# Two merge gates moved ahead of the GLA norm, a low-rank product moved behind the recurrence, another pace for w_ada, and a first expert turn of 64 slots with 21 first blocks

## The chip, the cores and the metric

The kernel runs on one core of one Trainium2 chip. The metric is the device time of one execution in microseconds; of several runs the median is taken. The core has a tensor engine (PE, with its weight loads as PEld), a vector engine (DVE), a scalar engine (ACT), GpSimd (POOL) and a sync engine (SP). SP issues nearly all weight transfers, POOL those of w_ada. A queue works its instructions in order, so one that waits holds up all behind it.

## The reference

Two layers of a decoder for 256 tokens of width 1024. Each has a token mixer and a channel mixer, both with a norm that a conditioning vector c scales and shifts (adaLN: six vectors per layer from `silu(c) @ w_ada`). The mixer runs a gated linear attention branch (GLA) and an RWKV-7 branch side by side and merges them with two sigmoid gates per channel:

```python
p = h @ w_in
y_a = _gla_branch(pq, pk, pv, pg, pa, ...)     # log_a from (pa @ alpha_up); o * rsqrt(mean(o*o)); silu(pg); @ w_o
y_b = _rwkv7_branch(p_rwkv, ...)               # recurrence over the tokens
merged = sigmoid(gate_a) * y_a + sigmoid(gate_b) * y_b
return merged @ w_out
```

`pa` has 16 columns: it is the low-rank gate input of the GLA decay. Layer 0's channel mixer is a dense SwiGLU of width 2816, layer 1's a mixture of 8 experts of width 3584 with the best 2 for each token. A token's expert output is weighted by a softmax over the two. A last norm closes the program.

## The kernel before, in words

All values are kept transposed, channels on partitions and the 256 tokens along the free axis. A weight block is 128 x 2048 f32, 1 MiB, and is called raw; `project` (L382) splits each 128 x 1024 half of it into hi and lo (L367 on ACT, L369 on DVE) and runs three matmuls per chunk of 128 (L392 to L394) into a PSUM tile pj, of which there are three. A projection over 1024 channels is 24 matmuls.

The order of the work comes from three sources. In the mixers and the dense layer a planner orders each engine's queue: it takes the instructions in the order of the text as priority, but pulls ahead what is ready when an engine would otherwise stand still. SP's queue is written out by hand there (LOADS), in the order of the text. In the expert stage the queues of PE, DVE, ACT and SP are all in the order of the text; a small clock (`tick`, `after`) places the side work between the products.

In `mixer` the text goes: projections W and G (L624 to L629), the low-rank gate product `pas` from wpa (L630 to L637: one split and 24 matmuls with 16 output columns), the low-rank RWKV products (L640 on), the RWKV projections, the recurrence (L776 to L817), its output yh and yl (up to L842), then the GLA branch: `decays()` (L865, reads pas at L871), `values` (L846), the heads and gates in the order of GATE_SEQ, the norm of the GLA output (`rsq` at L985, spread over partitions at L348, products at L992 to L994), four units of w_og (L996 to L1000), and eight merge steps (L1009 to L1019), each with a projection of a gate tile 38 + i, a tanh, a projection of w_or, and the merge; at last w_out.

The vectors from w_ada are made beside all this. A unit is 128 x 1024 of w_ada; POOL fetches it into one of two araw buffers (L230), DVE adds it to an accumulator (L254, L256), and after eight units two closing steps (`late`) finish a vector. `pace(n)` counts the chunks of each projection and calls `feed` for one unit or closing step each time PACE of the phase is full: 13 in mixer 0, 9 in the dense layer, 28 in mixer 1. `hold` stops it until the ninth entry of GATE_SEQ. `need(0, 4)` ahead of w_out in mixer 0 calls `feed` until vectors 2, 3 and 4 are there.

In `moe` the eight experts run in turns. Turn 0 is always expert 0, since its blocks are fetched before the router is known; the others are sorted by their token counts. A turn is small (CAP = 64 slots) or large (128 slots), by SMALL: before, turns 0, 2, 4, 6 are large and 1, 3, 5, 7 take the four experts with the fewest tokens. A turn has 7 steps j, each of 2 blocks for w1, w3 and w2: 42 blocks. A small turn multiplies the raw block in fp32 (L1404, L1423) with two column halves; a large one splits each half block (L1187, L1188) and runs three products (L1408 to L1410, L1426 to L1428). A large block is handed back when it is split, a small one when its products are done. `fetch` (L1163) issues blocks on SP: first the list FIRST, 18 places (15 raw ones and three that other tiles take over later: acts, late, y), then one for each block handed back while fewer than 15 are live. The expert order reaches SP through a register load (L1312). If a small turn has more than 64 tokens, or a large one more than 128, a branch at the end (`spill`) runs all experts again.

The places lie where mixer 1's tiles were, so the first transfers wait until these are done.

Of the kernel before, what the change touches and what calls it, by code (L numbers as in the profile page):

```python
# [9 lines left out]
F32 = mybir.dt.float32  # L10
F32R = mybir.dt.float32r
I32 = mybir.dt.int32
BF16 = mybir.dt.bfloat16
AF = mybir.ActivationFunctionType
# [4 lines left out]
P = 128  # L19
T = 256  # L20
# [37 lines left out]
NPRE = len(PRE)  # L58


RANK = [7, 0, 4, 1, 5, 2, 6, 3]
SMALL = [False, True] * 4
CAP = 64
NSMALL = sum(SMALL)
GROUPS = [(None, 0), (1, 2), (3, 4), (5, 6), (7, None)]


def constants():
# [367 lines left out]
WOUT = ((2, 'BT'), (3, 'TT'))  # L436
MOE_BUFS = 15
PLACES = [f"raw{i}" for i in range(6)] + ["acts", "late"] + [f"raw{i}" for i in range(6, MOE_BUFS)]
FIRST = ["acts", "late"] + [f"raw{i}" for i in (6, 7, 8, 4, 5, 12, 13, 14, 9, 10, 11, 2, 3, 1, 0)] + ["y"]
PACE = (13, 9, 28)  # L440
PACED_FROM = 8
ARAW_BUFS = 2
ARAW_WIDE = 6
# [86 lines left out]
def mixer(k, l):  # L530
# [10 lines left out]
    def g1():  # L541
        return made.pop() if made else dp.tile([P, T], F32, name="g1", bufs=G_BUFS)
# [45 lines left out]
    def tile_of(i):  # L588
        w = unit(i // 2)
        return w[:, (i % 2) * 1024:(i % 2) * 1024 + 1024]  # L590
# [36 lines left out]
    gds = shift(proj(1), 13)  # L627
    nc.scalar.activation(sgd, gds, AF.Tanh, scale=0.5)
    nc.vector.tensor_scalar(sgd, sgd, 0.5, 0.5, ALU.mult, ALU.add)  # L629
    hi, lo = k.split(wpa)  # L630
    pap = k.pj()
    for kc in range(KC):
        s = slice(kc * 16, kc * 16 + 16)
        nc.tensor.matmul(pap[:16, :T], hi[:, s], hh[:, kc, :], start=kc == 0, stop=False)
        nc.tensor.matmul(pap[:16, :T], hi[:, s], hl[:, kc, :], start=False, stop=False)
        nc.tensor.matmul(pap[:16, :T], lo[:, s], hh[:, kc, :], start=False, stop=kc == KC - 1)
    nc.scalar.activation(pas, pap[:16, :T], AF.Copy)  # L637


    PP, IP, AI, KK = [big[:, i * 1024:(i + 1) * 1024].rearrange("p (h t) -> p h t", h=4) for i in range(4)]  # L640
    for hp in range(2):
# [200 lines left out]
        nc.vector.tensor_tensor(yl[:, ht], u, yh[:, ht].bitcast(F32), ALU.subtract)  # L842

    def values(half):  # L846
        pv = [k.pj(), k.pj()]
# [134 lines left out]

    oh = dp.tile([P, 8, T], F32R, name="BK")
    ol = dp.tile([P, 8, T], F32R, name="vt")
    gsr = k.rsq(gss, 8, 1.0 / 256, 1e-5)  # L985
    for h in range(4):
        pb = k.pg()
# [19 lines left out]
        late[u] = dp.tile([P, 2048], F32, name=n)  # L1007
        nc.sync.dma_start(late[u], A["wout"][l, u])
    for i in range(8):  # L1009
        gb = k.project(tile_of(38 + i), act)  # L1010
        tb = g1()
        nc.scalar.activation(tb, gb, AF.Tanh, scale=0.5)
        if i % 4 == 0:
            w = k.raw(A["wor"][l, i // 4])
        py = k.project(w[:, (i % 4) * 512:(i % 4) * 512 + 512], (yh, yl))
        nc.vector.scalar_tensor_tensor(tb, tb, 1.0, py, ALU.add, ALU.mult)
        nc.vector.tensor_tensor(tb, tb, ta[:, i], ALU.add)
        nc.scalar.activation(mh[:, i], tb, AF.Copy, scale=0.5)
        nc.vector.scalar_tensor_tensor(ml[:, i], tb, 0.5, mh[:, i].bitcast(F32), ALU.mult, ALU.subtract)  # L1019
# [114 lines left out]
def moe(k, l, out):  # L1134
# [16 lines left out]
    todo = [o + (h,) for o in order for h in range(2)]  # L1151
    live, blocks, expert = [], [], [0]

    once = {n: sp.tile([P, 2048], F32, name=n) for n in PLACES}
    once["y"] = dp.tile([P, 2048], F32, name="y")
    slots = list(FIRST)

# [18 lines left out]
    def prepare(eng=nc.vector):  # L1176

        block = blocks[0]
        w, at, _ = block
        q = len(part)  # L1180
        s = slice(q * SUB, (q + 1) * SUB)
        last = q == 2048 // SUB - 1
        if SMALL[at[0]]:
            ready.append((w[:, s], None, at + (q,), block if last else None))
        else:
            hi, lo = [sp.tile([P, SUB], F32R, name=n, bufs=SPLIT_MOE) for n in ("hi", "lo")]
            nc.scalar.activation(hi, w[:, s], AF.Copy)  # L1187
            eng.tensor_tensor(lo, w[:, s], hi.bitcast(F32), ALU.subtract)  # L1188
            ready.append((hi, lo, at + (q,), None))
        part.append(q)  # L1190
        if last:
            part.clear()
            blocks.pop(0)
            if not SMALL[at[0]]:
                done(block)
# [6 lines left out]
            held[n] = sp.tile([P, 4, 512], kind, name=n)  # L1202
        return held[n]

    turns = [0, 0]

    def room():
        turns[0] += 1
# [82 lines left out]
    def sort():  # L1291

        by = lambda a: a[:, None, :].to_broadcast([P, NE, NE])
        of = lambda a: a[:, :, None].to_broadcast([P, NE, NE])
        p, w = perm[:, 0], perm[:, 1]

        def ranks():
            nc.vector.scalar_tensor_tensor(key, n8, 8.0, k.k("keyc"), ALU.mult, ALU.add)
            nc.vector.tensor_tensor(w, of(key), by(key), ALU.is_gt)
            nc.vector.tensor_reduce(rank, w, AX.X, ALU.add)  # L1300
            nc.vector.tensor_tensor(p, by(rank), of(k.k("seq")), ALU.is_equal)
            nc.vector.tensor_tensor(w, p, by(iota[:, :NE]), ALU.mult)
            nc.vector.tensor_reduce(idx, w, AX.X, ALU.add)
            nc.vector.tensor_copy(idxi, idx)

        def turned(src, dst):
            for tt in range(2):
                nc.vector.tensor_tensor(w, p, by(src[:, tt]), ALU.mult)
                nc.vector.tensor_reduce(dst[:, tt], w, AX.X, ALU.add)

        def loads():
            _, v = nc.values_load_multi_w_load_instructions(idxi[0:1, 1:NE], engines=[mybir.EngineType.SP], min_val=0,  # L1312
                                                            max_val=NE - 1)
            expert.extend(v)

        def excess():
            nc.vector.tensor_scalar(more, rank, NSMALL - 0.5, float(P - CAP), ALU.is_le, ALU.mult)
            nc.vector.tensor_tensor(n8, n8, more, ALU.add)
            nc.vector.tensor_reduce(cnt, n8, AX.X, ALU.max)
            nc.vector.tensor_copy(cnti, cnt)  # L1320

        return [ranks, loads, lambda: turned(posm, posm_s), lambda: turned(comb, comb_s), excess]
# [40 lines left out]

    def places(g):

        xs = dp.tile([P, KC, CAP], F32, name="xs") if GROUPS[g][0] is not None else None
        xl = [dp.tile([P, KC, P], F32R, name=n) for n in ("xh", "xl")] if GROUPS[g][1] is not None else None
        return xs, xl

# [225 lines left out]
    with tc.manual_schedule(engines=ORDERED | LOADS):  # L1595
        y = choose()
        idle = k.pj()
        busy(IDLE[0])
        pp = place()
        busy(IDLE[1])  # L1600
        for c in range(3):
            rows_of(c, y)
        rows_of(0, y, True)
        nc.vector.tensor_tensor(posm, posm, pp[:, 0:2 * NE].rearrange("p (a b) -> p a b", a=2), ALU.add)
        new = slots_of(0)
        nc.vector.tensor_copy(n8, pp[:, 2 * NE:3 * NE])
        rows_of(1, y, True)
        rows_of(2, y, True)
        to = places(0)
        for kc in range(KC):  # L1610
            gather(0, new[1], kc, to, k.pj if kc % 4 > 1 else k.pg)
        weigh()
        after(BACK, lambda: back(*new))
        for n, f in enumerate(sort()):
            after(SORT + n, f)
        group = new, to
        for e in range(NE):
            i = 0 if SMALL[e] else 1
            if e and i == 0:
                group = nxt  # L1620
            (_, _, gs, PT), (xs, x2) = group
            for j in range(NJ):
                ph = [k.pj()]
                up(e, j, 0, ph[0], x2 if i else xs)
                act, steps = hidden(e, ph)
                delay = DELAY
                if (e, j) == (NE - 1, NJ - 1):
                    delay, last = LAST, gains()
                after(delay[0], steps[0])
                ph.append(k.pj())  # L1630
                up(e, j, 1, ph[1], x2 if i else xs)
                for d, f in zip(delay[1:], steps[1:]):
                    after(d, f)
                if i == 1 and e < NE - 1:
                    g = e // 2 + 1
                    if j == NJ - 2:
                        new = slots_of(g)
                        after(BACK, lambda: back(*new))
                    if j == NJ - 1:
                        nxt = new, places(g)  # L1640
                        for kc in range(KC):
                            after(kc * 2048 // SUB // 4, lambda kc=kc, g=g, n=nxt: gather(g, n[0][1], kc, n[1]))
                if pend:
                    down(*pend[:4])
                    if pend[4]:
                        for d, f in in_turn(pend[0], *scatter(pend[0], pend[2], *pend[4])):
                            after(d, f)
                if j == 0:
                    py = []
                pend = (e, j, py, act, (gs[:, i:i + 1], PT, i) if j == NJ - 1 else None)  # L1650
        while tasks:
            tick()
        down(*pend[:4])
        banks = iter((k.pg, k.pg, k.pj, k.pj))
        finish(scatter(pend[0], pend[2], *pend[4], lambda: next(banks)()), *last)
# [168 lines left out]
```

## Time and profile before

| what | value |
|---|---|
| median of 3 runs | 1780.85 us (1779.85 to 1782.62) |
| profiled execution | 1777.78 us |
| its span, first to last instruction | 1776.0 us |
| granted TensorE clock, mean | 0.977 of 2.4 GHz |
| busy: PE, PEld, DVE, ACT, POOL | 96%, 79%, 65%, 47%, 3% |
| moved by DMA | 520.92 MB, mean 293 GB/s |

The profile is one execution on the chip. "Busy" of an engine is the union of its instructions; matmuls overlap, so the sum of their durations is more. A number behind a bar or in brackets is the engine's idle time just ahead of an instruction, with what ended it. PEclk is the granted clock as a share of 2.4 GHz. Mixer 0 ends near 357 us, the dense layer near 567, mixer 1 near 900; the expert stage follows.

### The profile page before, as it was taken

The page shows a single profiled execution, that of the slowest core. Times are in us where ns is not written, and L with a number is a line of the kernel's source. Part 1 is how long each engine was busy: PE and PEld are TensorE (multiplying, and loading weights), DVE is VectorE, ACT ScalarE, POOL GpSimd, SP SyncE. Part 2 cuts the span into 40 slices and gives each one's busy share as a digit, 9 for nine tenths or more (in the row PEclk, how much of TensorE's full clock was granted, in tenths as well). Part 3 has the DMA queues.
Part 4 walks back from the last instruction along what each step waited for, and adds up shares of the span by engine and source line. Part 5 has one row for each costly group of instructions (what it writes and reads, how often), then busy time and mean ns, then how long its engine had stood idle before and what let it go on. Part 6 is the DMA issues. An engine that isn't in the chain of part 4 may idle for free.

```text
span 1776.0 us, 30054 instructions
## 1 busy us (share of the span) xinstructions
PE 1703.6 (96%) x11915; PEld 1400.8 (79%) x11915; DVE 1161.7 (65%) x1783; ACT 838.2 (47%) x1214; POOL 50.3 (3%) x100
## 2 busy tenths in 40 slices
PE   7998989989999799999999999999999999999997
PEld 6987879989999688799977875688656876578754
DVE  3789577787876879466669950588407972289611
ACT  3653234454444743244547740477306771267501
POOL 0000010010100000000000000000000000000001
PEclk9999899999999899899989999999999999999999
DMA  9445257687874333225678989999999999999995
GB/s 347 158 165 190 73 182 259 249 287 304 314 267 145 110 129 119 73 96 190 261 307 311 366 314 421 421 421 421 418 420 421 421 421 416 421 421 421 420 421 214
DMA packets 79972, 520.92 MB, mean 293 GB/s; under 512 B 9520, under 2 KB 10160, under 8 KB 22352
## 3 DMA queue, kind: packets, MB, share of 16 engines
q1 hardware_dynamic: 67440, 476.14, 67.7%
q0 software_dynamic: 11232, 40.90, 6.7%
q8 instruction: 95, 1.56, 0.4%
q10 hardware_dynamic: 1152, 1.89, 0.3%
q14 instruction: 53, 0.43, 0.1%
HBM read 517.84 MB, written 1.05 MB: 292 GB/s over the span
## 4 chain that ended last, share of the span: by engine, by line
PE 76%; issue 8%; DMA 7%; DVE 6%; ACT 1%; POOL 0%; SPq 0%; ACTq 0%; POOLq 0%; DVEq 0%
PE pj L1404 11%; PE pj L392 7%; PE pj L393 7%; PE pj L394 7%; PE pc L1423 6%; PE pj L1408 5%; PE pj L1410 5%; PE pj L1409 5%; DMA araw<-wada 4%; PE pc L1426 3%; PE pc L1428 3%; PE pc L1427 3%; DMA raw<-moe 2%; PE pg L1453 1%; DVE lo L369 1%
## 5 line engine op out<-in xcount | busy, mean ns | idle before, releaser
L1188 DVE TENSOR_TENSOR lo<-raw,hi 128x1024 fp32r<-128x1024 f32 x330 | 396.1, 1223 | 85.0 <-ACT hi L1187 77.9
L1187 ACT ACTIVATE hi<-raw 128x1024 fp32r<-128x1024 f32 x330 | 347.5, 1059 | 128.1 <-PE pj L1409 80.0
L367 ACT ACTIVATE hi<-raw 128x1024 fp32r<-128x1024 f32 (+2 forms) x209 | 213.9, 1025 | 280.7 <-PE pj L393 207.6
L369 DVE TENSOR_TENSOR lo<-raw,hi 128x1024 fp32r<-128x1024 f32 (+2 forms) x209 | 246.5, 1181 | 77.5 <-ACT hi L367 73.9
L392 PE MATMUL pj<-hh,hi 128*128 128x256 f32 x992 | 289.9, 292 | 4.8 <-DVE t L418 3.4
L394 PE MATMUL pj<-hh,lo 128*128 128x256 f32 x992 | 285.9, 288 | 1.3 <-DVE lo L369 1.3
L393 PE MATMUL pj<-hl,hi 128*128 128x256 f32 x992 | 286.2, 289 | 0.0
L1404 PE MATMUL pj<-raw,xs 128*64 128x256 f32 x1792 | 201.4, 381 | 0.0
L392 PEld LDWEIGHTS pj<-hh,hi 128*128 128x128 f32 x992 | 191.2, 193 | 12.1 <-issue 4.8
L394 PEld LDWEIGHTS pj<-hh,lo 128*128 128x128 f32 x992 | 191.1, 193 | 2.5 <-DVE lo L369 1.8
L393 PEld LDWEIGHTS pj<-hl,hi 128*128 128x128 f32 x992 | 191.3, 193 | 2.2 <-issue 1.3
L1408 PE MATMUL pj<-hi,xh 128*128 128x512 f32 x448 | 181.3, 405 | 0.5 <-ACT hi L1187 0.5
L1410 PE MATMUL pj<-lo,xh 128*128 128x512 f32 x448 | 178.5, 398 | 2.0 <-DVE lo L1188 1.9
L1409 PE MATMUL pj<-hi,xl 128*128 128x512 f32 x448 | 177.7, 397 | 0.0
L1404 PEld LDWEIGHTS pj<-raw,xs 128*64 128x64 f32 x1792 | 125.8, 137 | 64.9 <-issue 4.7
L1448 DVE TENSOR_TENSOR late<-late,pj 128x512 f32<-128x512 f32 (+1 forms) x56 | 30.8, 550 | 207.6 <-PE pj L1404 201.0
L1410 PEld LDWEIGHTS pj<-lo,xh 128*128 128x128 f32 x448 | 84.5, 189 | 25.7 <-DVE lo L1188 5.4
L1423 PE MATMUL pc<-raw,as 128*64 128x512 f32 x448 | 102.2, 595 | 0.0
L1408 PEld LDWEIGHTS pj<-hi,xh 128*128 128x128 f32 x448 | 84.8, 189 | 21.2 <-ACT hi L1187 1.9
L1409 PEld LDWEIGHTS pj<-hi,xl 128*128 128x128 f32 x448 | 84.7, 189 | 18.7
L256 DVE SCALAR_TENSOR_TENSOR aacc<-araw,csg,aacc 128x1024 f32<-128x1024 f32 x70 | 89.6, 1280 | 8.0 <-DMA araw<-wada 7.5
L1426 PE MATMUL pc<-hi,acts 128*128 128x512 f32 x224 | 88.3, 394 | 0.0
(432 smaller groups left out, 2749.2 us busy)
## 6 DMA issues: line engine op xcount, KB each, us to landing
raw<-moe SPq DMA_DIRECT2D x333, 1024.0 KB, 18.6
raw<-win SPq DMA_DIRECT2D x43, 1024.0 KB, 5.0
araw<-wada POOLq DMA_DIRECT2D x78, 512.0 KB, 5.3
raw<-f SPq DMA_DIRECT2D x33, 1024.0 KB, 7.3
raw<-wv SPq DMA_DIRECT2D x8, 1024.0 KB, 4.8
raw<-wog SPq DMA_DIRECT2D x8, 1024.0 KB, 5.0
raw<-wad SPq DMA_DIRECT2D x6, 1024.0 KB, 7.1
raw<-wor SPq DMA_DIRECT2D x4, 1024.0 KB, 5.1
```

The lines of the kernel that those rows point to most:

```text
L367: nc.scalar.activation(hi[:, :w], src, AF.Copy)
L369: nc.vector.tensor_tensor(lo[:, :w], src, hi[:, :w].bitcast(F32), ALU.subtract)
L392: nc.tensor.matmul(o, hi[:, s], ah[:, kc, :], start=kc == 0, stop=False)
L393: nc.tensor.matmul(o, hi[:, s], al[:, kc, :], start=False, stop=False)
L394: nc.tensor.matmul(o, lo[:, s], ah[:, kc, :], start=False, stop=kc == nk - 1)
L1187: nc.scalar.activation(hi, w[:, s], AF.Copy)
L1188: eng.tensor_tensor(lo, w[:, s], hi.bitcast(F32), ALU.subtract)
L1404: nc.tensor.matmul(p[64 * n:64 * n + 64, :T], x[:, kc], hi[:, z * 512 + n * T:z * 512 + n * T + T], start=kc == 0, stop=kc == KC - 1)
L1408: nc.tensor.matmul(p, x[0][:, kc], hi[:, s], start=kc == 0, stop=False)
L1409: nc.tensor.matmul(p, x[1][:, kc], hi[:, s], start=False, stop=False)
L1410: nc.tensor.matmul(p, x[0][:, kc], lo[:, s], start=False, stop=kc == KC - 1)
L1423: nc.tensor.matmul(py[0][64 * n:64 * n + 64], act[:, a:a + CAP], hi[:, s], start=first, stop=last)
```

## The change

- `pas`, the low-rank gate product, moves from behind the projections W and G to behind yh and yl, ahead of `values` and `decays` in the text, in both mixers.
- Two of the eight merge gates (projection of tiles 38 and 39, and their tanh) move from the merge loop to ahead of the norm of the GLA output, in both mixers; so does the fetch of their unit, ahead of w_og's four on SP.
- PACE of mixer 0 goes from 13 to 10.
- Turn 0 becomes small: SMALL is true for turns 0, 1, 3, 5 and 7, and GROUPS, which pairs a small and a large turn for slots, places and gathers, is moved to match. Turn 1's tokens lie in a quarter of late, since turn 0's are still in use.
- The hi and lo tiles of the expert stage become three tiles hl0 to hl2 of the same total size, which serve as places for three more first blocks: 21 in place of 18.
- `excess` tests the ranks for the new set of small turns, with two more steps.

```diff
-SMALL = [False, True] * 4
+SMALL = [True] + [True, False] * 3 + [True]
-GROUPS = [(None, 0), (1, 2), (3, 4), (5, 6), (7, None)]
+GROUPS = [(0, None), (1, 2), (3, 4), (5, 6), (7, None)]
...
+FIRST = ["acts", "late"] + [f"raw{i}" for i in (6, 7, 8, 4, 5, 12, 13, 14, 9, 10, 11, 2, 3, 1, 0)] + ["y"] + [
+    f"hl{i}" for i in range(3)]
-PACE = (13, 9, 28)
+PACE = (10, 9, 28)
...
-    hi, lo = k.split(wpa)
-    pap = k.pj()
-    for kc in range(KC):
...
-    nc.scalar.activation(pas, pap[:16, :T], AF.Copy)
...
         nc.vector.tensor_tensor(yl[:, ht], u, yh[:, ht].bitcast(F32), ALU.subtract)
+    hi, lo = k.split(wpa)
+    pap = k.pj()
+    for kc in range(KC):
...
+    nc.scalar.activation(pas, pap[:16, :T], AF.Copy)
...
+    def merge_gate(i):
+        tb = g1()
+        nc.scalar.activation(tb, k.project(tile_of(38 + i), act), AF.Tanh, scale=0.5)
+        return tb
+
+    ahead = {i: merge_gate(i) for i in range(2)}
     gsr = k.rsq(gss, 8, 1.0 / 256, 1e-5)
...
-        gb = k.project(tile_of(38 + i), act)
-        tb = g1()
-        nc.scalar.activation(tb, gb, AF.Tanh, scale=0.5)
+        tb = ahead.pop(i) if i in ahead else merge_gate(i)
...
-    once = {n: sp.tile([P, 2048], F32, name=n) for n in PLACES}
+    once = {n: sp.tile([P, 2048], F32, name=n) for n in PLACES + [f"hl{i}" for i in range(SPLIT_MOE)]}
...
-            hi, lo = [sp.tile([P, SUB], F32R, name=n, bufs=SPLIT_MOE) for n in ("hi", "lo")]
+            hl = sp.tile([P, 2 * SUB], F32R, name=f"hl{turns[2] % SPLIT_MOE}")
+            turns[2] += 1
+            hi, lo = hl[:, :SUB], hl[:, SUB:]
...
-            nc.vector.tensor_scalar(more, rank, NSMALL - 0.5, float(P - CAP), ALU.is_le, ALU.mult)
+            nc.vector.tensor_scalar(more, rank, -5.0, None, ALU.add)
+            nc.vector.tensor_tensor(more, more, more, ALU.mult)
+            nc.vector.tensor_scalar(more, more, 2.0, float(P - CAP), ALU.is_ge, ALU.mult)
...
-        xs = dp.tile([P, KC, CAP], F32, name="xs") if GROUPS[g][0] is not None else None
+        xs = None
+        if g == 1:
+            xs = parts("late")[:, 3].rearrange("p (k n) -> p k n", k=KC)
+        elif GROUPS[g][0] is not None:
+            xs = dp.tile([P, KC, CAP], F32, name="xs")
...
-                if i == 1 and e < NE - 1:
+                if (i == 1 or e == 0) and e < NE - 1:
```

## Rows read from the trace of the kernel before

**Rows 1.** The page: engines' busy time, and GB/s in the 40 slices.
```profile
PE 1703.6 (96%) x11915; PEld 1400.8 (79%) x11915; DVE 1161.7 (65%) x1783; ACT 838.2 (47%) x1214; POOL 50.3 (3%) x100
...
GB/s 347 158 165 190 73 182 259 249 287 304 314 267 145 110 129 119 73 96 190 261 307 311 366 314 421 421 421 421 418 420 421 421 421 416 421 421 421 420 421 214
```

**Rows 2.** Windows, turns 0 to 2: length, busy by engine, PEclk, DMA share, GB/s.
```profile
916.20:1044.20 128.00, 124.14 (x562) 99.21 (x563) 107.60 (x132) 93.43 (x111) 0.00 (x0) 0.98 0.89 339
1044.20:1120.00 75.80, 75.80 (x566) 43.94 (x568) 12.76 (x21) 10.75 (x20) 0.00 (x0) 1.00 0.98 398
1120.00:1254.20 134.20, 132.83 (x622) 102.93 (x619) 109.61 (x115) 95.09 (x112) 0.00 (x0) 1.00 1.01 421
```

**Rows 3.** Windows by transfer: opening of the expert stage, steady part, tail.
```profile
898.30:1053.30 155.00, 148.20 (x711) 118.90 (x711) 126.26 (x187) 106.44 (x134) 0.00 (x0) 0.97 0.88 338
1053.30:1754.80 701.50, 697.57 (x4068) 480.14 (x4069) 373.54 (x416) 322.33 (x404) 2.90 (x8) 1.00 1.01 418
1754.80:1776.00 21.20, 11.44 (x84) 8.42 (x80) 6.01 (x18) 4.68 (x8) 2.19 (x3) 0.86 0.15 54
```

**Rows 4.** Timeline of SP's queue, and one row of ACT: start, us, instruction.
```profile
210.54 50.43 SPq L379 DMA_DIRECT2D raw<-wog  x4
...
898.26 8.90 SPq L1163 DMA_DIRECT2D raw<-moe  x10
...
905.25 2.04 ACT L1187 ACTIVATE hi<-acts 128x1024 fp32r<-128x1024 f32 x2
...
909.31 0.33 SPq L1163 DMA_DIRECT2D y<-moe  x1
924.60 136.51 SPq L1163 DMA_DIRECT2D raw<-moe  x45
```

**Rows 5.** Timeline of the tensor engine in both mixers; idle time ahead in brackets.
```profile
95.58 0.51 PE L858 MATMUL pj<-hi,hh 128*128 128x512 f32 x1
...
128.51 0.71 PE L904 MATMUL pg<-g,g 128*128 128x128 f32 x4
...
260.70 0.44 PE L278 MATMUL ada<-cst,sq 128*128 128x128 f32 x2 [1.23 <-ACT sq L273]
265.71 2.08 PE L348 MATMUL pg<-cst,rsq 128*128 128x128 f32 x8 [4.57 <-DVE rsq L341]
...
586.69 0.37 PE L634 MATMUL pj<-hh,hi 128*16 128x256 f32 x1 [7.81 <-DVE t L418]
...
811.55 0.62 PE L392 MATMUL pj<-BK,hi 128*128 128x256 f32 x3 [0.71 <-ACT BK L993]
```

**Rows 6.** Instructions of one line: SP's read of the order (L1312), block transfers (L1163).
```profile
L1312 SPq TENSOR_LOAD <-idxi x1: 1663/1663/1663, 934.5 to 934.5; - x1
...
DMA to landing us min/median/max: 5.0/18.6/20.8
```

**Rows 7.** Windows for the matmul's price and the granted clock.
```profile
930.00:940.00 10.00, 8.02 (x34) 5.45 (x34) 9.12 (x20) 6.61 (x7) 0.00 (x0) 1.00 0.34 116
...
264.70:271.60 6.90, 5.72 (x25) 5.43 (x26) 5.44 (x15) 2.43 (x6) 0.82 (x2) 0.51 1.01 419
...
400.00:500.00 100.00, 100.00 (x846) 98.37 (x846) 76.47 (x85) 43.72 (x59) 12.69 (x24) 1.00 0.84 316
```

**Rows 8.** Timeline of DVE in the mixers.
```profile
259.35 1.22 DVE L369 TENSOR_TENSOR lo<-raw,hi 128x1024 fp32r<-128x1024 f32 x1
...
290.31 1.28 DVE L256 SCALAR_TENSOR_TENSOR aacc<-araw,csg,aacc 128x1024 f32<-128x1024 f32 x1 [3.07 <-DMA araw<-wada]
...
576.20 1.28 DVE L256 SCALAR_TENSOR_TENSOR aacc<-araw,csg,aacc 128x1024 f32<-128x1024 f32 x1
```

**Rows 9.** Waits: engine and line waited for, us in total, times, longest.
```profile
POOL araw L230 <- DVE aacc L256: 108.2, 41, 10.6
```

**Rows 10.** Windows of the recurrences, instructions on the accumulators pj alone.
```profile
128.50:234.10 105.60, 56.81 (x349) 49.27 (x349) 4.22 (x10) 3.84 (x9) 0.92 0.41 140
672.90:758.80 85.90, 47.07 (x272) 38.55 (x270) 2.54 (x6) 3.44 (x8) 0.90 0.28 97
```

More of the change, by code (lines that the diff above doesn't have):

```diff
@@ L61 @@
 RANK = [7, 0, 4, 1, 5, 2, 6, 3]
-SMALL = [False, True] * 4
+SMALL = [True] + [True, False] * 3 + [True]
 CAP = 64
-NSMALL = sum(SMALL)
-GROUPS = [(None, 0), (1, 2), (3, 4), (5, 6), (7, None)]
+GROUPS = [(0, None), (1, 2), (3, 4), (5, 6), (7, None)]
 def constants():
@@ L438 @@
 PLACES = [f"raw{i}" for i in range(6)] + ["acts", "late"] + [f"raw{i}" for i in range(6, MOE_BUFS)]
-FIRST = ["acts", "late"] + [f"raw{i}" for i in (6, 7, 8, 4, 5, 12, 13, 14, 9, 10, 11, 2, 3, 1, 0)] + ["y"]
-PACE = (13, 9, 28)
+FIRST = ["acts", "late"] + [f"raw{i}" for i in (6, 7, 8, 4, 5, 12, 13, 14, 9, 10, 11, 2, 3, 1, 0)] + ["y"] + [
+    f"hl{i}" for i in range(3)]
+PACE = (10, 9, 28)
 PACED_FROM = 8
@@ L629, in mixer @@
     nc.vector.tensor_scalar(sgd, sgd, 0.5, 0.5, ALU.mult, ALU.add)
-    hi, lo = k.split(wpa)
-    pap = k.pj()
-    for kc in range(KC):
[L633 to L636, printed above, removed]
-    nc.scalar.activation(pas, pap[:16, :T], AF.Copy)
     PP, IP, AI, KK = [big[:, i * 1024:(i + 1) * 1024].rearrange("p (h t) -> p h t", h=4) for i in range(4)]
@@ L842, in mixer @@
         nc.vector.tensor_tensor(yl[:, ht], u, yh[:, ht].bitcast(F32), ALU.subtract)
+    hi, lo = k.split(wpa)
+    pap = k.pj()
+    for kc in range(KC):
+        s = slice(kc * 16, kc * 16 + 16)
+        nc.tensor.matmul(pap[:16, :T], hi[:, s], hh[:, kc, :], start=kc == 0, stop=False)
+        nc.tensor.matmul(pap[:16, :T], hi[:, s], hl[:, kc, :], start=False, stop=False)
+        nc.tensor.matmul(pap[:16, :T], lo[:, s], hh[:, kc, :], start=False, stop=kc == KC - 1)
+    nc.scalar.activation(pas, pap[:16, :T], AF.Copy)
     def values(half):
@@ L1203, in parts @@
         return held[n]
-    turns = [0, 0]
+    turns = [0, 0, 0]
     def room():
```

## The prediction

> **What bounds the kernel now.** I read the page's slices first, then the expert stage turn by turn, the transfers there, and the tensor engine's holes in the mixers. The tensor engine is busy for 96% of the span [rows 1], nearly everywhere, so its share does not say what ends last; the slices' GB/s do. From slice 25 on they stand at 416 to 421 but for the last, and lower and uneven before.
>
> In the expert stage the reader should compare two prices of a turn (one expert, 42 blocks of 1 MiB, 44.04 MB). A large turn (128 slots, hi/lo split, three products) takes 134.2 us of the tensor engine, a small one (64 slots, raw weights) 75.8 [rows 2]. From 1053.3 us to the last landing at 1754.8 the queue moves 418 GB/s [rows 3], so 42 blocks take 44.04 MB / 418 GB/s = 105.4 us. A pair takes 134.2 + 75.8 = 210.0 us of products and 210.8 of transfer: from the second turn on **the transfers are the bound**, and the engine is as busy only because a pair is balanced to them. The first turn is the one expert stretch where they are not: it is large, starts with all buffers full and hands blocks back only as it splits them, so the queue gets 339 GB/s [rows 2]. From 898.3, where the rest of the first blocks is issued [rows 4], to 1053.3 the mean is 338 [rows 3].
>
> In the mixers the tensor engine is the bound between short holes: 1.23 and 4.57 us around the GLA output's norm in layer 0, 7.81 at layer 1's start [rows 5].
>
> **The change part by part.**
>
> *First turn of 64 slots, 21 first blocks.* Five small and three large turns are 5 x 75.8 + 3 x 134.2 = 782 us of products in place of 840, but 336 blocks still need 8 x 105.4 = 843 of transfer. So the 58 us saved on the engine are not the gain; the gain is the transfer time that the first turn wasted. In 155.0 us at 338 GB/s the queue moved what takes 155.0 x 338 / 418 = 125.3: **29.7 us to win**, if it never runs dry from 898.3 on. The 21.2 us behind the last landing [rows 3] stay.
>
> Does it run dry? A small turn uses a block every 75.8 / 42 = 1.80 us, a transfer takes 105.4 / 42 = 2.51. Before, y was the last of 18 first blocks, issued at 909.3, and the next came only at 924.6 [rows 4]. The ten blocks from 898.3 and y land until about 898.3 + 5.0 [rows 6] + 10 x 2.5 = 928; hl0 to hl2 carry the queue 7.5 us on, to 936. They lie where hi and lo lay, which ACT first wrote at 905.2 [rows 4], so they can be issued right behind y; on SP all later blocks and the read of the experts' order queue behind them. Products start at about 916 as before [rows 2], or a little earlier, since DVE is rid of three splits; the third block is used by 916 + 3 x 1.8 = 921, or by 927 at half clock, and its successor must be issued 5.0 us before 936. Between them SP reads the experts' order, 1.66 us and seven register steps [rows 6], held up before by splits ahead of it on DVE, which are gone. That is some 4 us of slack: I charge nothing, and each us beyond it costs one. The engine catches up with the landings after some 40 blocks and then waits 0.7 us per block, which costs nothing. In each large turn it falls 134.2 - 105.4 = 29 us behind, 11.5 blocks of 15; the later large turn at 421 GB/s shows that this fits [rows 2]. Bounds 0 and -29.7; I take **-29.7**, since the queue's later rows are nearest. Turn 1's tokens in a quarter of late, and two more short steps in excess(), fall into DVE time that the splits leave free: 0.
>
> A rule speaks against this part. The row first: between 930 and 940 the engine was busy 8.02 of 10 us and its granted clock stayed 1.00 (2.4 GHz); behind the hole of 4.57 us it was half, 1.2 GHz [rows 7]. Waits of 0.7 in 2.5 us are nearest to the first of these. The Trainium skill, "TensorE: Matmul & The Clock Gate", section on HAM oscillation, says that thin products which wait for each transfer lose the full clock again and again. No row here shows a starved small turn, so the trace leaves that open; by the row this part stays at -29.7, by the rule it becomes rival D.
>
> *Two merge gates ahead of the GLA norm.* A projection is 24 matmuls of 100 / 846 = 0.118 us [rows 7], 2.8 us; two cover 5.7 of the holes' 1.23 + 4.57. The half clock behind, 6.9 us [rows 7], cost up to 3.4 more. Against that their two lo's of 1.22 us [rows 8] join the norm's short steps on DVE. On SP their unit goes ahead of w_og's four loads, each of which then waits one buffer longer; they were issued from 210.5 on [rows 4], far ahead of the norm, so nothing. Bounds +2.4 and -9.2; I take **-5**. In layer 1 the hole there is 0.71 us [rows 5]: 0 (bounds +2.4, -0.7).
>
> *Low-rank gate product behind the recurrence.* 24 matmuls, 2.8 us, leave the place between layer 1's hole of 7.81 us [rows 5] and the low-rank products that start the RWKV chain, likewise in layer 0, with a split on ACT and DVE. They must be paid elsewhere. Bounds per layer: -2.8 if a hole takes them, +2.8 if the early place was hidden and the late one is not; I take -1.5 each, **-3**. Their cover is the planner's: values(), also behind the recurrence in the text, runs from 95.6 us on [rows 5], far ahead of it.
>
> *w_ada's pace 10.* Ahead of need(0, 4) mixer 0 passes 320 paced chunks: 32 feeds in place of 24, where 30 are due; six forced feeds become spread ones, and some three units leave later stages. A unit costs DVE 1.28 us wherever it stands [rows 8], and POOL's issue waited for DVE 41 times [rows 9]. Gain: two units stand just ahead of layer 1's norm, the second at 576.2, and partly go, and the stall of 3.07 us may go [rows 8]. Loss: two buffers that turn over faster can bring three more such stalls. Bounds -6 and +9; I take **-1.5**.
>
> **Sum**: -29.7 - 5 - 3 - 1.5 = -39. The profiled execution took 1777.78 us (its span of 1776.0 and 1.8 around it), 3.1 less than the median of 1780.85. 1777.8 - 39 = 1738.6, and for the median **1741**.
>
> **Rivals.**
>
> *A. The mixers give their 9.5 us back.* The planner orders anew whatever stands behind an edit, and a feed or a lo in the wrong place stalls a chain of short steps. The first turn's 29.7 remain and the mixers cost 0 to 10 us: 1751 to 1761. For it: the bounds above reach +9 and +2.4. Against: the hole of 4.57 us is there to be filled.
>
> *B. The queue still runs dry in the first turn.* If the order is read late again, or the hl places come free late, half the gain is lost: about 1756. For it: the gap from 909.3 to 924.6 [rows 4]. Against: DVE's splits, which caused it, are gone.
>
> *C. Slower: the gate product really waits for the recurrence.* decays() needs it, all GLA heads need decays(), and the first head's product runs at 128.5 [rows 5]. Then a q projection holds its accumulator until the recurrence ends, and the projections that fill the recurrence stop: 56.8 us of them in layer 0, 47.1 in layer 1 [rows 10], unhidden behind it: up to 104 - 39 = 65 us slower, 1846. It decides from 39 us on. Against: values() at 95.6.
>
> *D. Slower: the clock halves in the starved turns.* Products could end at 916 + 782 = 1698, the last landing comes at 1754.8 - 29.7 = 1725: 27 us of slack and 29.7 of gain are 57 us that the engine can lose before the old time is reached, three quarters of one small turn at 1.2 GHz. Two whole ones lose 152: 95 slower but for the mixers' 9.5, 1866. Against: an engine at half clock needs 3.6 us for a block that lands every 2.5, so it no longer waits. The Trainium skill's rule above speaks for it.
>
> *E. The change does not hold: expert 0 has more than 64 tokens.* Then the spill branch runs all experts again in two passes, 16 x 105.4 = 1686 us more, about 3430. The reference's router gives expert 0 60 tokens on its inputs.
>
> **How the numbers follow.** Forecast (1730 to 1751): 0.62. A: 0.22. B: 0.08. C: 0.04. D: 0.03. E: 0.01. The range goes down to 1729, all the mixers' lower bounds together (-21.5 on 1751), and up through B and A to 1760; outside lie C, D, E and the edges of the rest, at most 2 in 10. A measurement of this kernel tells 0.2%, 3.6 us, from no change. Faster: forecast, A and B but for a sliver, 0.91; same: 0.02; slower: C, D, E, 0.07 with rounding.
>
> **What would show it.** Right: 416 to 421 GB/s from about 900 us to the last landing, and that landing 30 us nearer to the issue of the ten blocks; turns 0 and 1 near 105 us each, with short waits for transfers and a granted clock of 1.00; holes at layer 0's norm below 1.5 us together; the low-rank gate product near 95 us. Wrong: a dip in GB/s 35 to 40 us behind the ten blocks' issue (B); the first GLA head later than 160 us (C); clock 0.5 through the first two turns (D); the ten blocks' issue later than 898 (A).

## The result, and the profile after

The changed kernel takes **1755.26 us** (median of 4 runs, 1752.64 to 1759.52), the one before, run beside it, 1780.96: a ratio of 0.9857, 95% interval 0.9836 to 0.9878. That is 1.4% faster, inside the range, and 14 us above the forecast of 1741, at the place where rival A puts it (1751 to 1761). The profiled execution took 1752.64 us, 25.1 less than that of before.

The page of the changed kernel, engines and GB/s, answers to [rows 1]:

```profile
PE 1663.8 (95%) x11957; PEld 1338.9 (76%) x11957; DVE 1054.9 (60%) x1684; ACT 749.1 (43%) x1129; POOL 50.8 (3%) x100
...
GB/s 336 176 156 179 111 133 253 282 269 309 294 313 165 104 97 121 74 97 173 203 287 421 421 421 421 421 421 421 419 420 421 420 415 420 421 420 421 416 421 209
```

421 GB/s begins with slice 22, that is at 919 us; before it took until slice 25, at 1066. What that is worth stands in the windows (columns as in [rows 2]): turn 0 and turn 1 as the tensor engine runs them, the starved part of turn 1, then the stretch from the opening of the ten blocks to the last landing, and the tail.

```profile
914.00:994.60 80.60, 80.00 (x609) 45.26 (x608) 11.41 (x48) 11.73 (x35) 0.00 (x0) 1.00 1.01 421
994.60:1096.30 101.70, 84.69 (x591) 42.12 (x590) 6.18 (x15) 7.04 (x17) 0.00 (x0) 1.00 1.01 421
...
1021.50:1096.30 74.80, 58.22 (x394) 28.25 (x394) 2.11 (x5) 4.53 (x11) 0.00 (x0) 1.00 1.01 421
...
901.30:1728.50 827.20, 802.85 (x4814) 537.72 (x4815) 392.55 (x504) 339.21 (x452) 2.90 (x8) 1.00 1.01 418
1728.50:1750.80 22.30, 13.22 (x90) 9.26 (x86) 6.01 (x18) 4.69 (x8) 2.19 (x3) 0.79 0.15 52
```

So the 25 us fall into three parts. From the opening to the last landing it is 827.2 us; before it was 1754.8 - 898.3 = 856.5 [rows 3]: **29.3 us less**, where I had forecast 29.7. The tail is 22.3 against 21.2 [rows 3], 1.1 more, at a granted clock of 0.79 instead of 0.86. And the opening itself, forecast 9.5 us earlier, comes **3.0 us later**: 901.30 against 898.26 [rows 4], as SP's queue shows.

```profile
901.30 8.92 SPq L1169 DMA_DIRECT2D raw<-moe  x10
912.39 0.33 SPq L1169 DMA_DIRECT2D y<-moe  x1
914.88 5.29 SPq L1169 DMA_DIRECT2D hl<-moe  x3
925.34 4.87 SPq L1169 DMA_DIRECT2D raw<-moe  x4
```

The expert stage did what was forecast; in these two profiles the mixers missed by 12.5 us. (Single openings carry little: two executions of one program open 8 us apart, as a later section shows.) The tensor engine's timeline in the mixers, with idle time ahead in brackets, answers to [rows 5]:

```profile
51.84 0.39 PE L392 MATMUL pj<-hh,hi 128*128 128x256 f32 x1 [0.70 <-ACT hi L367]
...
53.10 0.39 PE L394 MATMUL pj<-hh,lo 128*128 128x256 f32 x1 [0.76 <-DVE lo L369]
...
65.65 0.36 PE L392 MATMUL pj<-hh,hi 128*128 128x256 f32 x1 [1.45 <-DVE t L622]
...
95.93 0.28 PE L841 MATMUL pj<-hh,hi 128*16 128x256 f32 x1
...
135.70 0.71 PE L906 MATMUL pg<-g,g 128*128 128x128 f32 x4 [1.60 <-DVE g L898]
...
272.30 1.05 PE L348 MATMUL pg<-cst,rsq 128*128 128x128 f32 x8
...
303.23 0.36 PE L392 MATMUL pj<-hh,hi 128*128 128x256 f32 x1 [1.74 <-DVE ta L1008]
...
380.93 0.55 PE L392 MATMUL pj<-hh,hi 128*128 128x256 f32 x1 [4.02 <-DVE t L418]
...
592.75 0.55 PE L392 MATMUL pj<-hh,hi 128*128 128x256 f32 x1 [6.25 <-DVE t L418]
...
608.53 0.58 PE L392 MATMUL pj<-hh,hi 128*128 128x256 f32 x1 [3.73 <-DVE t L418]
```

The norm's spread (L348, at 272.30) has no hole ahead of it any more, where 1.23 and 4.57 us stood in [rows 5]. But three holes of 2.9 us together have opened between 51 and 66 us, right where the low-rank gate product was taken out, and in layer 1 a hole of 3.73 us follows the 6.25 that remain of 7.81.

### The profile page after: what moved, and what is told of

Read it like the earlier page. It is cut to its first block, busy times and chain, and to the rows that moved or that the text cites. A ratio compares the mean times of both kernels' runs of the same rounds, so it can differ in the third digit from the quotient of the medians.

```text
span 1750.8 us, 29702 instructions
## 1 busy us (share of the span) xinstructions
PE 1663.8 (95%) x11957; PEld 1338.9 (76%) x11957; DVE 1054.9 (60%) x1684; ACT 749.1 (43%) x1129; POOL 50.8 (3%) x100
## 4 chain that ended last, share of the span: by engine, by line
PE 75%; DVE 10%; DMA 10%; issue 2%; ACT 2%; SPq 0%; ACTq 0%; POOL 0%; DVEq 0%; POOLq 0%
PE pj L1418 11%; PE pj L392 7%; PE pj L393 7%; PE pj L394 7%; DMA raw<-moe 7%; PE pc L1437 6%; PE pj L1424 4%; PE pj L1422 4%; PE pj L1423 4%; DVE lo L369 2%; DMA araw<-wada 2%; PE pc L1440 2%; PE pc L1442 2%; PE pc L1441 2%; PE pg L1467 1%
## 5 line engine op out<-in xcount | busy, mean ns | idle before, releaser
L1196 DVE TENSOR_TENSOR hl<-raw,hl 128x1024 fp32r<-128x1024 f32 x252 | 303.2, 1223 | 74.5 <-ACT hl L1195 68.6
L1195 ACT ACTIVATE hl<-raw 128x1024 fp32r<-128x1024 f32 x252 | 265.7, 1060 | 115.1 <-PE pj L1424 61.0
L1462 DVE TENSOR_TENSOR late<-late,pj 128x256 f32<-128x256 f32 (+1 forms) x56 | 29.0, 518 | 281.9 <-PE pj L1418 276.1
L1422 PE MATMUL pj<-hl,xh 128*128 128x512 f32 x336 | 135.4, 403 | 1.3 <-ACT hl L1195 1.3
L1424 PE MATMUL pj<-hl,xh 128*128 128x512 f32 x336 | 133.2, 396 | 0.6 <-DVE hl L1196 0.5
L1437 PE MATMUL pc<-raw,as 128*64 128x512 f32 x552 | 127.6, 596 | 5.6 <-DMA raw<-moe 5.6
L1423 PE MATMUL pj<-hl,xl 128*128 128x512 f32 x336 | 132.7, 395 | 0.0
L1470 ACT ACTIVATE as<-pg 128x256 f32<-128x256 f32 x35 | 13.4, 383 | 207.8 <-PE pg L1467 207.8
L256 DVE SCALAR_TENSOR_TENSOR aacc<-araw,csg,aacc 128x1024 f32<-128x1024 f32 x70 | 89.7, 1281 | 11.2 <-DMA araw<-wada 10.8
L1437 PEld LDWEIGHTS pc<-raw,as 128*64 128x64 f32 x552 | 38.0, 137 | 70.8 <-issue 58.1
L392 PE MATMUL pj<-BK,hi 128*128 128x256 f32 (+1 forms) x280 | 79.9, 291 | 1.9 <-ACT BK L1024 1.1
L393 PE MATMUL pj<-vt,hi 128*128 128x256 f32 (+1 forms) x280 | 78.9, 286 | 0.5 <-DVE vt L1025 0.5
## 6 DMA issues: line engine op xcount, KB each, us to landing
raw<-moe SPq DMA_DIRECT2D x330, 1024.0 KB, 19.8
```

The lines of the kernel that those rows point to most:

```text
L392: nc.tensor.matmul(o, hi[:, s], ah[:, kc, :], start=kc == 0, stop=False)
L393: nc.tensor.matmul(o, hi[:, s], al[:, kc, :], start=False, stop=False)
L1422: nc.tensor.matmul(p, x[0][:, kc], hi[:, s], start=kc == 0, stop=False)
L1423: nc.tensor.matmul(p, x[1][:, kc], hi[:, s], start=False, stop=False)
L1424: nc.tensor.matmul(p, x[0][:, kc], lo[:, s], start=False, stop=kc == KC - 1)
L1437: nc.tensor.matmul(py[0][64 * n:64 * n + 64], act[:, a:a + CAP], hi[:, s], start=first, stop=last)
```

## The experiments

All of them keep the expert stage's change unless it is said otherwise; diffs are against the changed kernel. Two questions: does the expert stage gain for the reason given, and which edit cost the mixers their 12.5 us?

### The expert stage: the three extra first blocks, and the first turn

```diff
-    f"hl{i}" for i in range(3)]
+FIRST = ["acts", "late", ..., "y"]                   # 18
```

> The changed kernel with 18 first blocks: hl0 to hl2 are no longer loaded behind y. Read from the opening of the ten blocks to the last landing, which is 827 us in every kernel with the small first turn so far. If the three extra blocks carry the queue as the prediction has it (7.5 us of transfers that nothing else would fill): 834 to 835. If the next block's issue at about 925 us comes in time for most of that, because y itself lands only near 932: 827 to 830.

Measured: one run, 1753.44 us; opening 902.5, last landing 1729.6, so **827.1 us**, no loss at all. SP's queue in that kernel:

```profile
902.48 9.00 SPq L1168 DMA_DIRECT2D raw<-moe  x10
913.63 0.33 SPq L1168 DMA_DIRECT2D y<-moe  x1
920.65 13.88 SPq L1168 DMA_DIRECT2D raw<-moe  x8
```

y lands 19.8 us after its issue, at 933.4, and the next block is on its way from 920.65, long before that. The extra places carry nothing that would otherwise be lost.

```diff
-SMALL = [True] + [True, False] * 3 + [True]
+SMALL = [False, True, False, True, False, True, True, True]
...
-    f"hl{i}" for i in range(3)]
```

> The changed kernel with 18 first blocks, three large turns as in the change, but the first turn large: large, small, large, small, large, small, small, small (one expert with 69 tokens runs in 64 slots, so its last five tokens are left out). It has the 58 us fewer products and not the small first turn. Theory T (transfers are the bound, and only the first turn wasted any): from the opening of the ten blocks to the last landing 855 to 859 us, as before with 856.5, and the total 28 to 30 us above the changed kernel. Rival (fewer products are what shortened the stage): 827 to 831 us.

Measured: one run, 1783.39 us. The window from the opening to the last landing, and SP's queue:

```profile
905.30:1761.60 856.30, 817.34 (x4858) 543.32 (x4857) 391.25 (x505) 340.75 (x453) 2.89 (x8) 1.00 0.99 404
```

```profile
905.30 9.12 SPq L1169 DMA_DIRECT2D raw<-moe  x10
916.58 0.33 SPq L1169 DMA_DIRECT2D y<-moe  x1
931.39 16.89 SPq L1169 DMA_DIRECT2D raw<-moe  x5
```

The kernel also leaves out the test that sends experts with too many tokens to the spill branch. 856.3 us, as before the change, although this kernel has the same three large turns and the same 782 us of products as the changed one. The next block goes out at 931.39, 14.8 us behind y, much as before (909.31 and 924.60 in [rows 4], 15.3 us). In one run of each kernel, and far beyond the 1 us by which this window varies, that settles it: the 58 us of products buy nothing, the small turn at the *first* place buys the 29.

### Each mixer edit undone

```diff
-PACE = (10, 9, 28)
+PACE = (13, 9, 28)
```

> The changed kernel with w_ada's pace back at 13, all else as changed. The mixers opened the ten blocks 3.0 us later than before where I forecast 9.5 us earlier, and three edits could carry that. Theory P (the gate product's late place makes decays() and with it the GLA heads late): the time stays within 2 us of the changed kernel's 1755. Theory W (32 feeds in mixer 0 instead of 24, whose buffers come late, stall DVE and with it the heads): the time falls by 6 to 9 us, to 1746 to 1749, the last GLA head's norm sum comes near 250 us instead of 260, and DVE waits for the feeds' buffers nearer to 7.5 than to 10.8 us. Theory G (the merge gates' splits hold up the heads' end): within 2 us of 1755.

Measured: 1758.69 us, ratio 0.9877 (0.9857 to 0.9896). Slower if anything, and above what any of the three theories gave: theory W falls. DVE's waits for the feeds' buffers are longer here (13.6 us, 9 times) than in the changed kernel (10.8, 8 times).

```diff
     nc.vector.tensor_scalar(sgd, sgd, 0.5, 0.5, ALU.mult, ALU.add)
+    hi, lo = k.split(wpa)
+    pap = k.pj()
...
-    hi, lo = k.split(wpa)
-    pap = k.pj()
...
     def values(half):
```

> The changed kernel with the low-rank gate product back at its early place, all else as changed. Theory P: the decays' products come near 63 us again, the first GLA head near 128.5 instead of 135.7, and the time falls by 6 to 9 us, to 1746 to 1749. Theory W: within 2 us of 1755, since the feeds stay as many. Theory G: within 2 us of 1755.

Measured: **1751.16 us**, ratio 0.9822 (0.9800 to 0.9844). The direction and most of the size of theory P. The tensor engine around the product's early place, in both layers:

```profile
51.29 0.28 PE L637 MATMUL pj<-hh,lo 128*16 128x256 f32 x1
51.49 0.48 PE L645 MATMUL pc<-t,sm 64*128 64x256 f32 x1
...
63.79 1.56 PE L873 MATMUL pg<-pas,al 16*128 16x256 f32 x6
...
590.30 0.37 PE L635 MATMUL pj<-hh,hi 128*16 128x256 f32 x1 [6.24 <-DVE t L418]
...
604.91 1.34 PE L873 MATMUL pg<-pas,al 16*128 16x256 f32 x5
...
616.01 0.58 PE L392 MATMUL pj<-hh,hi 128*128 128x256 f32 x1 [1.64 <-DVE t L622]
```

No bracket stands at 51 and at 64 us: the product, and behind it the decays' products that it sets free (L873), lie over the steps of ACT and DVE for which the changed kernel waits 0.70, 0.76 and 1.45 us. In layer 1 they stand at 590 and 605, where it waits 3.73; here 1.64 us of waiting are left at 616, which the changed kernel does not have.

```diff
-    ahead = {i: merge_gate(i) for i in range(2)}
...
-        tb = ahead.pop(i) if i in ahead else merge_gate(i)
+        gb = k.project(tile_of(38 + i), act)
```

> The changed kernel with all eight merge gates back in the merge loop, all else as changed. Theories P and W: the holes of 1.23 and 4.57 us around layer 0's norm come back with the half clock behind, and the time rises by 4 to 6 us, to 1759 to 1761. Theory G: the last head's norm sum comes near 250 us instead of 260 and the time falls by 4 to 8 us, to 1747 to 1751.

Measured: 1754.58 us, ratio 0.9870 (0.9847 to 0.9894). Neither: with pace 10 and the product late, the gates' place makes no difference that shows.

All three mixer edits undone:

> The kernel before with the change to the expert stage alone (first turn of 64 slots, 21 first blocks); gates, gate product and pace as before. Every theory of the mixers gives the opening of the ten blocks at 898.3 us, as before, and 827 us from there to the last landing: 1781.0 - 29.3 + 1.1 (the tail measured in the changed kernel) = 1752.8. If the expert stage gains only with the other edits (rival B in another form), it is above 1757.

Measured: 1755.55 us (4 runs), ratio 0.9864 (0.9844 to 0.9885). The profiled execution opened at 897.9, and its last landing came 827.0 us later, as expected; its time was 1749.5, the lowest of the four. The median lies between the two expectations.

### Each mixer edit alone, and the changed kernel again

> The expert stage's change and the two gates ahead; gate product early, pace 13. My forecast's term for the gates is 5 us: 1755.6 (the expert stage alone) - 5 = 1750.6. Theory H (the mixers' idle time is conserved: a hole that is filled opens again at the next chain of short steps, since the engine only reaches it sooner): the holes of 1.23 and 4.57 us are gone, others at 297 to 380 us grow, idle time of the tensor engine ahead of the ten blocks stays within 2 us of the 40.7 of the expert stage alone, and the time is 1754 to 1757.

Measured: 1748.64 us, ratio 0.9823 (0.9801 to 0.9845). The time is the forecast's, while the idle time is theory H's: 40.4 us.

> The expert stage's change and pace 10; gates in their loop, gate product early. If pace 10 helps by itself (the changed kernel against the same with pace 13: 3.4 us): 1752. If what that pair showed lies in which stretches ran at half clock and not in the feeds: 1754 to 1757, with DVE's stalls for the feeds' buffers no shorter than before.

Measured: 1748.91 us, ratio 0.9826 (0.9806 to 0.9847). DVE waits 11.2 us for the feeds' buffers, 6 times, where it was 7.5 and 4 times before: pace 10 does not win by shorter stalls.

> The expert stage's change and the gate product behind the recurrence; gates in their loop, pace 13. Theory P (at its early place the product sat in a hole of the tensor engine, late it is paid): idle time in the first 100 us rises from 0.9 (expert stage alone) to between 3.5 and 5, the opening of the ten blocks comes 2 to 5 us later than 897.9, time 1757 to 1760. My forecast's term: 3 us earlier, time 1752 to 1753. If run-to-run spread is all there is: 1754 to 1757.

Measured: **1764.29 us**, ratio 0.9914 (0.9894 to 0.9933). The slowest of all, by more than theory P said. Its idle time in the first 100 us is 4.65 us, within what theory P gave.

> The changed kernel unaltered, beside the three above on the same chip, for a second profile of it: how much of the mixers' differences one profile can carry. Median 1754 to 1757. If the spread between profiles of one kernel is small, its opening of the ten blocks is at 901.3 within 1 us and its stretches at half clock ahead of it sum to 61 within 3 us; if it is large, idle time is again near 44.6 but the half clock's sum differs by more than 5 us and the opening moves by half of that.

Measured: 1757.59 us, ratio 0.9887 (0.9865 to 0.9908).

### Without the gate product, and the expert stage alone again

```diff
+    nc.vector.memset(pas, 0.0)
...
-    hi, lo = k.split(wpa)
...
```

> The changed kernel without the low-rank gate product at all (its result is set to zero, so the decays come from the bias alone); gates ahead, pace 10. Beside it stand the product early (1751.2) and late (1755.3 and 1757.6). If the early place was hidden in a hole of the tensor engine: 1749 to 1752, as with the product early, with idle time in the first 100 us near 4.5 as with the product late. If the early place costs its 2 x 2.8 us like any other: 1744 to 1747, and the late place then costs only what lies beyond that.

Measured: 1753.43 us, ratio 0.9863 (0.9843 to 0.9883). 48 matmuls fewer than with the product early, and no faster (1751.16), where the product's own 5.6 us would show: at its early place the product costs nothing that shows. Idle time in the first 100 us is 4.1 us, near the 4.5 of the first expectation.

> The expert stage's change alone, once more, since the verdicts on gates and pace hang on it (1748.6 and 1748.9 against its 1755.6, from four runs). If gates and pace each gain 6 to 7 us by themselves: 1754 to 1757 again. If its four runs lay high: 1750 to 1753, and gates and pace gain 2 to 4.

Measured: 1753.89 us, ratio 0.9853 (0.9834 to 0.9872): just below the first expectation; with the four runs above, the median of eight is 1754.3.

### Reading them together

The windows from 24 us to the opening of the ten blocks show what the tensor engine does there; length less PE's busy time is its idle time. First the expert stage alone, two executions of one program:

```profile
24.00:100.00 76.00, 75.14 (x688) 68.98 (x678) 54.17 (x112) 47.05 (x88) 0.95 (x1) 1.00 0.60 220
24.00:897.90 873.90, 833.16 (x6920) 782.19 (x6909) 653.25 (x1146) 398.26 (x655) 43.38 (x80) 0.96 0.53 190
```

```profile
24.00:100.00 76.00, 75.42 (x699) 69.43 (x691) 54.18 (x112) 47.34 (x88) 0.96 (x1) 1.00 0.60 220
24.00:906.00 882.00, 841.16 (x6932) 790.29 (x6923) 653.64 (x1146) 398.76 (x655) 43.55 (x80) 0.95 0.52 188
```

Idle 40.7 and 40.8 us, busy 833.2 and 841.2, opening 897.9 and 906.0. The work is the same; the 8 us between them are matmuls at the lower clock (0.96 and 0.95 in the mean). Now the changed kernel, its own profile and the second one:

```profile
24.00:100.00 76.00, 71.16 (x672) 65.77 (x665) 52.53 (x110) 42.85 (x80) 0.95 (x1) 1.00 0.58 208
24.00:901.30 877.30, 832.70 (x6924) 779.05 (x6916) 653.45 (x1146) 398.56 (x655) 43.88 (x80) 0.96 0.53 189
```

```profile
24.00:100.00 76.00, 72.00 (x667) 66.42 (x657) 53.58 (x111) 44.12 (x82) 0.95 (x1) 1.00 0.58 216
24.00:905.40 881.40, 837.45 (x6911) 782.52 (x6900) 653.01 (x1145) 398.65 (x655) 43.71 (x80) 0.96 0.52 189
```

Idle 44.6 and 44.0, of it 4.8 and 4.0 in the first 100 us, against 0.9 and 0.6 in the expert stage alone; busy 832.7 and 837.5. So in these two pairs **idle time repeats to within 1 us, busy time moves by 5 to 8 us from one execution to the next**. Over more executions idle time scatters by 2 to 3 us: the kernels with 18 first blocks and with the large first turn have the changed kernel's mixers, and 45.0 and 46.7 us; the kernel before has those of the expert stage alone, and 43.1. By idle time up to the opening, the kernels still fall into two groups: 40.7, 40.8, 40.4, 41.6 and 39.5 us with the product early (expert stage alone twice, gates, pace, both) and 43.1 before the change; 47.9, 45.6, 43.7, 44.6 and 44.0 with it late, besides the 45.0 and 46.7.

The granted clock parts them further. Length times (1 - granted clock), taken over windows of 20 us from 24 us to the opening and added up, estimates the time that the lower clock cost; it is an estimate, since it treats the engine as what sets the pace throughout. It gives 34 and 43 us for the two executions of the expert stage alone, which accounts for the 8 us between them. With it taken off, **the opening comes at 861.8 to 865.7 us in the six profiles with the product early and at 868.1 to 872.7 in the seven with it late**, 6.7 us later in the mean; 4.3 of these are idle time, 2.4 busy time. Neither the gates alone (864.0) nor pace 10 alone (863.3) moves it from the expert stage alone (863.9 and 863.0).

The medians (the expert stage alone from its 8 runs, the changed kernel from its 9) form a table, late less early in the last column:

| gates | pace | product early | product late | late costs |
|---|---|---|---|---|
| in the loop | 13 | 1754.3 | 1764.3 | 10.0 |
| ahead | 13 | 1748.6 | 1758.7 | 10.1 |
| in the loop | 10 | 1748.9 | 1754.6 | 5.7 |
| ahead | 10 | 1751.2 | 1756.7 | 5.5 |

One ratio is known to about 0.002, so a single difference only to about 5 us. But all four pairs say that the product's late place costs, 7.8 us in the mean. Gates ahead are worth 5.6 or 5.7 us at pace 13 and lose 2.1 or 2.3 at pace 10, in both columns; pace 10 wins 5.4 and 9.7 with the gates in the loop, and 2.0 or minus 2.6 with them ahead. One by one, these stand little above what a single difference is known to. And what gates alone and pace alone gain came with a higher granted clock: 0.9776 and 0.9786 in the mean of their five runs each, 0.9735 in the eight of the expert stage alone, which at 1750 us is 7 to 9 us. The kernel before, beside them, had 0.9760 and 0.974, so whether the edits raise the clock or the runs fell out so is not shown.

**Better than both kernels** are the three with the product early and at least one of the other edits: 1748.6 to 1751.2, some 5.5 to 8 us below the changed kernel. Among the three the runs do not decide.

## Why the prediction was right or wrong

**First turn of 64 slots: right, in sign, place and size.** Forecast -29.7, measured -29.3 in the profile, and from 827.0 to 827.9 us from the opening to the last landing in every kernel with it. The reason held too: the large-first kernel has the products of the change and the transfers of before, and takes 856.3.

**21 first blocks: no part of it.** The prediction put the empty queue at 928 without the extra places, and the next issue between 921 and 927 plus the read of the order. y landed about where it said (932.3 in a kernel that opens 3.0 us later), but the release came at the early end, since the clock never fell in that turn: with 18 first blocks the next one goes out at 920.65. I had taken the three blocks as a condition of the 29.7 without pricing the case without them.

**Engine against landings: nearly.** Turn 0 runs for 80.6 us ahead of the transfers and turn 1 takes the rest, not 105 us each. The engine reaches the landings at about 1021 us, behind some 55 blocks in place of 40, and then waits, as the rows of turn 1 show:

```profile
1022.01 1.95 PE L1418 MATMUL pj<-raw,late 128*64 128x256 f32 x16 [0.53 <-DMA raw<-moe]
1024.60 1.95 PE L1418 MATMUL pj<-raw,late 128*64 128x256 f32 x16 [0.64 <-DMA raw<-moe]
1026.99 1.95 PE L1418 MATMUL pj<-raw,late 128*64 128x256 f32 x16 [0.45 <-DMA raw<-moe]
```

**Low-rank gate product: wrong, and the term that decides.** Forecast -3, measured +5.5 to +10. The step that failed is "I take -1.5 each": between the bounds of -2.8 and +2.8 I went to the side of the hole of 7.81 us *ahead* of the product in layer 1 [rows 5], and read it as time that the product stands in the way of. But that hole is waited out whatever comes first behind it: it is 6.24 us with the product early and 6.25 with it late. What mattered was what the product covers *behind* itself. In layer 0 that is 2.9 us of holes that were not there to be seen, because it filled them: the three (0.70, 0.76 and 0.98 to 1.49) stand in every profile with the product late and in none with it early. In layer 1 less is new than the 3.73 us at 608 suggest: with the product early 1.64 us stand at 616 instead, so about 2 are new with pace 10, and with pace 13 about half a microsecond (3.10 late, 1.13 and 1.42 early). The kernel without the product shows it from the other side: 5.6 us of work less, and no less time. The upper bound, "the early place was hidden and the late one is not", was the case; it gives +5.6. Of the 6.7 us by which the opening comes later once the cost of the clock is taken off, near the 7.8 of the medians, idle time is 4.3; the other 2.4 are busy time, and why the same products are busy that much longer no run shows.

**Two merge gates: the hole went as forecast, but pace 10 fills it too.** Forecast -5. Alone they give -5.7 in the medians, next to pace 10 they give +2. One reason stands in the rows of the norm's spread, first with the gates alone, then with pace 10 alone:

```profile
267.68 1.16 PE L348 MATMUL pg<-cst,rsq 128*128 128x128 f32 x8 [0.95 <-DVE rsq L341]
...
262.81 1.05 PE L348 MATMUL pg<-cst,rsq 128*128 128x128 f32 x8
```

Of the hole of 4.57 us the gates leave 0.95, and pace 10 nothing with all gates in their loop, so there is no second gain to add. Nor does the sum of idle time fall by much with the gates (40.4 against 40.7 and 40.8): the engine reaches the next chain of short steps sooner and waits there, 0.82 and 1.21 us at 298 and 301 us for w_og's last sums. The -5.7 of the medians is not in the opening once the clock is taken off; it came with the clock that these runs were granted.

**w_ada's pace: size missed.** Forecast -1.5 within -6 and +9; alone -5.4, next to the gates +2.6 or -2.0. One part of the gain came as forecast: of the two units ahead of layer 1's norm one is left, at 581.96 us in the changed kernel, and the hole of 7.81 us is 6.24 or 6.25. The stall that was to go did not: DVE's waits for the buffers grew from 7.5 us to 10.8 in the changed kernel and 11.2 with pace 10 alone. And pace 10 opens a hole that I had not looked for, ahead of the dense layer's first normed result; again with the gates alone, then with pace 10 alone:

```profile
374.06 0.36 PE L392 MATMUL pj<-hh,hi 128*128 128x256 f32 x1 [0.74 <-DVE t L418]
...
379.77 0.55 PE L392 MATMUL pj<-hh,hi 128*128 128x256 f32 x1 [4.01 <-DVE t L418]
```

It is the 4.02 us at 381 in the changed kernel. In all, the idle time is no less with pace 10 alone (41.6 us), and the gain in the medians came with the clock, as with the gates.

**Sum.** By the medians: expert stage -26.3 (1754.3 against some 1780.6), gates and pace together -3.1, product +5.5, in all -24 against a forecast of -39. (By its own terms the forecast was 1741.7, written as 1741.) The parts that missed are the product (8.5 off), the overlap of gates and pace (3.4) and, in the medians, the expert stage (29.7 against 26.3: 1.1 to 1.6 of it the tail, the rest within the scatter of the mixers' clock).

**Rivals.** A came true, though not through a feed or a lo in a wrong place. The sign that I had set for it, an opening later than 898, could not have told: the expert stage alone opens at 897.9 and at 906.0. B fell: no dip behind the ten blocks, not even with 18 first blocks (419 to 426 GB/s in each 10 us from 10 to 60 us behind the issue). C fell: the product runs at 95.93, not behind the recurrence, and the first GLA head at 135.70, far from 160. D fell: in 74.8 us at 78% busy, with a wait for each block, the granted clock stayed 1.00, that is 2.4 GHz. The Trainium skill, "TensorE: Matmul & The Clock Gate", section on HAM oscillation, tells of a loop whose products are shorter than the wait for the next transfer. Here it is the other way round, 1.95 us of products and waits of 0.45 to 0.64, so the row neither bears that rule out nor speaks against it: the prediction had applied it without its condition.

## What to carry to other kernels

A short product behind a hole is not in the way of what follows: ask what it covers, by finding what its successors wait for, before you move it, and price its removal from its place as well as its arrival elsewhere. When a queue of transfers is the bound, look for the one stretch where it isn't full; the work saved elsewhere is worth nothing, as three large turns instead of four showed. And when several small edits are judged in a stretch whose clock moves, take the cost of the lower clock off first, and compare the tensor engine's idle time between profiles, which moved by 2 to 3 us here, ahead of single openings, which moved by 8.

## What the runs showed of the hardware

The same program spends 833.2 us or 841.2 us of tensor engine time on the same matmuls, in two executions, on two chips. The chip alone does not make such a difference: four executions on the first one ran from 1749.48 us, at a mean clock of 0.976, to 1756.98, at 0.971. The largest piece of the difference lies at the recurrence of layer 0. In both executions the engine waits there 1.74 us for the same instruction of DVE; here are that row and the window behind it (granted clock third from the right), for the first execution of the expert stage alone and then for the second:

```profile
188.46 1.73 PE L760 MATMUL pc<-TW,big 32*32 32x32 f32 x49 [1.74 <-DVE TW L753]
...
188.00:210.00 22.00, 21.54 (x271) 20.06 (x272) 11.64 (x16) 6.70 (x11) 0.00 (x0) 0.77 0.15 49
```

```profile
188.02 2.18 PE L760 MATMUL pc<-TW,big 32*32 32x32 f32 x46 [1.74 <-DVE TW L753]
...
188.00:210.00 22.00, 21.98 (x234) 20.66 (x235) 9.56 (x13) 4.90 (x9) 0.00 (x0) 0.53 0.15 48
```

Behind the same hole the mean clock is 0.77 of 2.4 GHz in one and 0.53, nearly all at 1.2 GHz, in the other: 22 x (0.77 - 0.53) = 5.3 us of full clock in this stretch alone. Nor does a busy engine mean a full clock: in the second execution it was busy for 21.98 of these 22 us. I had treated the half clock behind a hole as a price that belongs to the hole. Here it does not, what decides it no run shows, and the 8 us are more than any of the mixer edits was forecast to move.
